# A one-core two-block kernel: gates of layer 0 in another order, and expert weights by rounded products

## The chip, the cores and the metric

The kernel runs on one core of one Trainium2 chip. The metric is the device time of one execution in microseconds (us). Five engines work beside each other: TensorE (PE, matrix products; PEld is its loading of weights), VectorE (DVE), ScalarE (ACT), GpSimd (POOL) and SyncE (SP), which issues most of the transfers. Each follows its own list of instructions, which is fixed when the program is built, and they wait for each other by semaphores.

## The reference

256 tokens of width 2048 pass a first block of two layers, then a second block. Layer 0 is attention next to a convolution, each with a gate:

```python
k, v, q, za, glu, zb = jnp.split(h @ w_in, EV_SPLITS, axis=-1)
...
attn = latent_attention(q, k, v, kc, vc)
conv = conformer_conv(glu, ev_dw_w[e], ev_dw_b[e], ev_ln_g[e], ev_ln_b[e])
mix = jnp.concatenate([attn * jax.nn.silu(za), conv * jax.nn.silu(zb)], axis=-1)
x_new = x + gate * (mix @ ev_w_out[e])
```

Layer 1 is a spatial gating unit. The second block adds a state space mixer, causal attention, and a layer of 16384 single-neuron experts, of which each token picks 8 heads x 16:

```python
q = (h @ w_q).reshape(bsz, seq, PEER_HEADS, 2, PEER_HALF_DIM)
scores = jnp.einsum('bshpd,hpnd->bshpn', q, sub_keys).astype(jnp.float32)
sv, si = lax.top_k(scores, PEER_TOPK)
...
gw = jax.nn.softmax(tv, axis=-1).astype(h.dtype)
...
a = jnp.einsum('td,ted->te', xc, expert_u[ic])
a = jax.nn.gelu(a, approximate=False) * wc
return jnp.einsum('te,ted->td', a, expert_v[ic])
```

## The kernel before

**Products.** All weights are F32 and come from DRAM in chunks of 1 MB, each half of which is 128 x 1024 numbers. ScalarE rounds a half to `whi` (fp32r, the rounded form that TensorE multiplies at full rate), VectorE makes the rest, `wlo` = raw - `whi`. The activations are split in the same way, and three rounded products make one F32 product: high by high, high by low, low by high. The text calls the products of half a chunk a half. `gemm` keeps the weights in place and streams 256 columns of tokens; `gemm_tok` keeps the tokens in place and streams 512 columns of weights; `gemm_pairs` (for `pu`, the first expert matrix) keeps the weights in place and streams high and low tokens as 512 columns for `whi`, and 256 for `wlo`.

**Order.** A planner at build time (the clock and its prices, with `SYNC`, `TICK`) calls the threads (Python generators) in turn: `add` and `post` put a thread into the plan, `fill` runs what is due after each half, `finish` runs a thread to its end there and then. A `yield "d"` hands over to VectorE's due time, `"a"` to ScalarE's, `"p1"` to TensorE's, and `"w"` waits for something else. So the order of instructions on each engine follows from prices, not from arrival at run time. The raw chunks have a ring of buffers; three `wlo` can wait unused. The long sums of the modulation vectors (`ada`) are used as filler, on TensorE (`adaps`) or on VectorE (`adaacc`).

**Layer 0.** `EV_ORDER` is the order of column groups of the first weight matrix: 1, 2, 3 are convolution input, 5 and 6 queries, 7 and 8 the gate of the convolution (`gate_b`), 9 and 10 the gate of attention (`gate_a`). A gate is computed by tokens, put through Silu by ScalarE (`szt`) and transposed by TensorE (`turn`). `attended` multiplies it into the attention result and splits that into `mixs`; `conv_ln` finishes the convolution's half. Then `evo`, the output product, runs in two passes over its inner dimension, the attention's half first. `mixed` holds the threads of the two attention groups, and `self.finish(*mixed)` stands ahead of the first evo product, `self.finish(ln)` ahead of the second pass.

**Experts.** `peer` computes the queries `pq` (four groups), scores them, and finds the 16 best of each head (`topk`, mostly VectorE). All 16384 experts are then computed densely: `pu` gives 256 x 16384 activations, which GELU and a dense matrix of weights (0 for experts not chosen) turn into `A`, and `pv` multiplies that by the second matrix. `PEER_ORDER` lists the pieces: `u` 0 to 13 first (104 halves of `pu`), then `v` 0 to 4, and so on.

The dense weights come from `expert_weights` and `weight_products`. A token's weights are a 128 x 128 matrix, the product of two one-hot matrices over its 128 choices, one of them scaled by the choice's weight. For each of 64 groups of four tokens, VectorE makes both (`oneh`, from the transposed choices `selT`: plane 1 against the numbers 0 to 127, then plane 0 with plane 2 as the weight), TensorE multiplies them into `pw`, ScalarE copies that to `wst`, and after each eight groups SP stores them to DRAM (`wd`). `weigh` loads them back by expert (`wrd`), VectorE multiplies `raw_a`, the GELU's result, by them, and ScalarE and VectorE split the product into `As`, on which `pv` waits. `RING` is how many groups of one-hot tiles may be ready. Every load `wrd` takes a slice of all eight stores, so the first one needs the last store.

In the trace every instruction stands at line 409, the helper that records it, so tiles are read by name.

## Time and profile before

| | |
|---|---|
| time, three runs | 3151.94, 3152.35, 3160.5 us; median 3152.35 |
| profiled execution | 3148.4 us, span of the core 3146.6 us |
| TensorE busy | 3080.5 us, 98% of the span |
| VectorE busy | 2263.6 us, 72% |
| ScalarE busy | 1496.6 us, 48% |
| DMA | 762.61 MB, mean 242 GB/s |
| chain that ended last | PE 90%, DVE 6%, ACT 2%, DMA 1% |

All times in what follows are of the profiled execution, counted from the start of the span. Busy time alone doesn't say what a change is worth: matrix products overlap by some hundred ns, so the distance from one start to the next is their price, not the length of one. Idle time is given with what ended it. A stretch of the chain of waits gives, in order of time, the work that nothing else could have covered.

### The profile page before, as it was taken

The numbers are of one execution on the slowest core, as the hardware profiler recorded it, in microseconds if no ns is written. First come the engines' busy times: TensorE is split into PE (matmuls) and PEld (weight loads), VectorE is DVE, ScalarE is ACT, GpSimd is POOL, SyncE is SP. The second block draws the span as 40 slices with busy tenths as digits, with TensorE's granted clock in tenths as the row PEclk, the third lists the DMA queues.
The fourth block names the chain that finished last, engine by engine and source line by source line (L and its number), as shares of the span: only waits on it lengthen the run. The fifth ranks groups of instructions, "written<-read, shape, count | busy, mean of one in ns | idle before, by whom it ended". The sixth has DMA issues, their size and how long they took to land.

```text
span 3146.6 us, 43549 instructions
## 1 busy us (share of the span) xinstructions
PE 3080.5 (98%) x17104; PEld 2562.6 (81%) x17104; DVE 2263.6 (72%) x3457; ACT 1496.6 (48%) x2044; POOL 12.7 (0%) x25
## 2 busy tenths in 40 slices
PE   6899999999999999999999999999999999999999
PEld 5666779778897777789998898888888888888887
DVE  4499879788777887868789997555566556655654
ACT  3345554445445556544445555444354444444433
POOL 0000000000000000000000000000000000000000
PEclk8999999999999999999999999999999999999999
DMA  8877786788875565777654566566566666655663
GB/s 341 331 282 256 257 308 225 280 320 316 304 291 201 221 239 185 271 276 285 243 181 174 190 239 242 208 219 207 201 242 234 228 219 250 237 207 205 232 214 134
DMA packets 140781, 762.61 MB, mean 242 GB/s; under 512 B 12624, under 2 KB 45392, under 8 KB 53920
## 3 DMA queue, kind: packets, MB, share of 16 engines
q1 hardware_dynamic: 137680, 750.83, 65.3%
q0 software_dynamic: 1744, 5.85, 0.6%
q8 instruction: 134, 2.20, 0.3%
q10 hardware_dynamic: 1152, 3.15, 0.3%
q14 instruction: 71, 0.58, 0.1%
HBM read 738.81 MB, written 20.97 MB: 241 GB/s over the span
## 4 chain that ended last, share of the span: by engine, by line
PE 90%; DVE 6%; ACT 2%; DMA 1%; issue 1%; SPq 0%; ACTq 0%; DVEq 0%
PE pv L409 25%; PE q L409 23%; PE pu L409 21%; PE ps L409 9%; PE adaps L409 3%; DVE wlo L409 2%; PE last L409 2%; PE pw L409 2%; PE S L409 1%; PE kvc L409 1%; PE kv L409 1%; DVE si L409 1%; PE po L409 1%; PE ss L409 0%; PE turn L409 0%
## 5 line engine op out<-in xcount | busy, mean ns | idle before, releaser
L409 DVE TENSOR_TENSOR wlo<-raw,whi 128x1024 fp32r<-128x1024 f32 x970 | 1177.2, 1220 | 563.4 <-PE pv L409 270.4
L409 ACT ACTIVATE whi<-raw 128x1024 fp32r<-128x1024 f32 x970 | 1022.8, 1060 | 1118.5 <-PE pv L409 396.2
L409 PE MATMUL pu<-hs,whi 128*128 128x512 f32 x2048 | 725.1, 398 | 0.0
L409 PE MATMUL q<-whi,hs 128*128 128x512 f32 x1984 | 643.6, 397 | 3.9 <-DVE ypad L409 3.9
L409 PE MATMUL pv<-whi,As 128*128 128x512 f32 x2048 | 633.6, 390 | 0.8 <-DVE y L409 0.8
L409 PE MATMUL pu<-hs,wlo 128*128 128x256 f32 x2048 | 574.7, 281 | 1.2 <-DVE wlo L409 1.2
L409 PEld LDWEIGHTS q<-whi,hs 128*128 128x128 f32 x1984 | 373.5, 188 | 120.6 <-issue 34.1
L409 PEld LDWEIGHTS pu<-hs,whi 128*128 128x128 f32 x2048 | 384.6, 188 | 91.0
L409 PEld LDWEIGHTS pv<-whi,As 128*128 128x128 f32 x2048 | 384.5, 188 | 81.6 <-DVE y L409 1.2
L409 PE MATMUL pv<-wlo,As 128*128 128x512 f32 x1024 | 398.4, 389 | 0.0
L409 PE MATMUL q<-wlo,hs 128*128 128x512 f32 x992 | 388.5, 392 | 0.9 <-DVE wlo L409 0.9
L409 PEld LDWEIGHTS pu<-hs,wlo 128*128 128x128 f32 x2048 | 386.8, 189 | 2.8 <-DVE wlo L409 2.6
L409 DVE SCALAR_TENSOR_TENSOR adaacc<-raw,silc,adaacc 128x1024 f32<-128x1024 f32 x176 | 221.2, 1280 | 101.8 <-DMA raw<-in_ada_dram 101.7
L409 PEld LDWEIGHTS pv<-wlo,As 128*128 128x128 f32 x1024 | 192.3, 188 | 40.9 <-issue 1.0
L409 PEld LDWEIGHTS q<-wlo,hs 128*128 128x128 f32 x992 | 187.1, 189 | 39.7 <-DVE wlo L409 3.3
L409 PE MATMUL ps<-hs,whi 128*128 128x256 f32 x768 | 152.3, 298 | 21.8 <-ACT hs L409 17.0
L409 PE MATMUL ps<-mixs,whi 128*128 128x256 f32 x832 | 154.7, 288 | 0.0
L409 PEld LDWEIGHTS ps<-hs,whi 128*128 128x128 f32 x768 | 126.8, 202 | 29.3 <-ACT hs L409 21.1
L409 PEld LDWEIGHTS ps<-mixs,whi 128*128 128x128 f32 x832 | 132.5, 196 | 3.5 <-issue 3.4
L409 PE MATMUL ps<-mixs,wlo 128*128 128x256 f32 x416 | 119.1, 286 | 0.0
L409 PE MATMUL ps<-hs,wlo 128*128 128x256 f32 x384 | 113.0, 294 | 1.2 <-DVE wlo L409 1.2
L409 DVE SCALAR_TENSOR_TENSOR cacc<-ypad,pk,cacc 128x256 f32<-128x256 f32 x240 | 99.3, 477 | 0.0
(382 smaller groups left out, 3045.6 us busy)
## 6 DMA issues: line engine op xcount, KB each, us to landing
raw<-in_ada_dram SPq DMA_DIRECT2D x160, 1024.0 KB, 5.2
raw<-in_pu_dram SPq DMA_DIRECT2D x128, 1024.0 KB, 4.9
raw<-in_pv_dram SPq DMA_DIRECT2D x128, 1024.0 KB, 4.8
raw<-in_w_dram SPq DMA_DIRECT2D x60, 1024.0 KB, 4.8
raw<-in_od_dram SPq DMA_DIRECT2D x48, 1024.0 KB, 6.8
raw<-in_ev_dram SPq DMA_DIRECT2D x44, 1024.0 KB, 5.4
raw<-in_ada0s_dram SPq DMA_DIRECT2D x32, 1024.0 KB, 7.9
raw<-in_evo_dram SPq DMA_DIRECT2D x16, 1024.0 KB, 5.2
```

The source lines that it names most:

```text
L409: r = f(*args, **kw)
```

## The change

Four edits. (1) In layer 0 the attention gates (9, 10) are computed ahead of the convolution's gates (7, 8), and the mixture is a `LazySplit`: each part is finished when the first product that reads it is written down, not ahead of all. (2) In `gemm_pairs` each half does its eight products with `whi`, then its eight with `wlo`, instead of alternating. (3) `pq` is computed by tokens (`gemm_tok`, 384 products of 512 columns instead of 768 of 256), copied out by ScalarE, transposed by TensorE (32 transposes) and copied again. (4) The one-hot tiles are rounded numbers now: 0 and 1 are exact, and the weight is split into a rounded part (plane 3) and the rest (plane 2). VectorE makes four tiles of 128 x 512 for four tokens: `oneh`, the unscaled `onew`, and its products with the two weight planes, both of which read the unscaled tile, the second in place. TensorE does two rounded products of 128 columns for each token instead of one F32 product. `RING` falls from 4 to 2.

```diff
@@ -173,10 +173,10 @@
 PEER_ORDER = (("u", 0, 13), ("v", 0, 4), ("v", 4, 8), ("v", 8, 12), ("u", 13, 20), ("v", 12, 18), ("u", 20, 26), ("v", 18, 24),
               ("u", 26, 32), ("v", 24, 32))
 SPARE = 2
-RING = 4
+RING = 2
 LAG = 2
 GATE_AT = 120
-EV_ORDER = (1, 2, 5, 6, 3, 7, 8, 9, 10)
+EV_ORDER = (1, 2, 5, 6, 3, 9, 10, 7, 8)
 
 
 def make_plan():
@@ -691,12 +691,11 @@
         for kc in range(n_kc):
             for j in range(2):
                 hi, lo = (t.rearrange("p a (b n) -> p (a b) n", n=256) for t in self.take(name, g, kc, j))
-                for a in range(4):
-                    kt = 8 * kc + 4 * j + a
-                    for n in range(2):
-                        s = slice(n * 128, n * 128 + 128)
-                        self.mm(ps[:, n], hi[:, a, s], act.hl(kt), start=(kt == 0), stop=False, skip_group_check=True)
-                        self.mm(ps[:, n, 1, :], lo[:, a, s], act.h(kt), start=False, stop=(kt == 8 * n_kc - 1), skip_group_check=True)
+                part = [(a, n, 8 * kc + 4 * j + a, slice(n * 128, n * 128 + 128)) for a in range(4) for n in range(2)]
+                for a, n, kt, s in part:
+                    self.mm(ps[:, n], hi[:, a, s], act.hl(kt), start=(kt == 0), stop=False, skip_group_check=True)
+                for a, n, kt, s in part:
+                    self.mm(ps[:, n, 1, :], lo[:, a, s], act.h(kt), start=False, stop=(kt == 8 * n_kc - 1), skip_group_check=True)
                 self.fill()
         return ps
 
@@ -1235,7 +1234,7 @@
                 heads.append(self.add(self.attn0(4 * g + j, qT[g][:, j, :], kT, V, at[g][:, j, :], [t] + tk, st), 2))
 
         szb = [None] * 2
-        mix = Split()
+        mix = LazySplit(self)
 
         def silu(t, ps):
 
@@ -1260,7 +1259,7 @@
 
         def gate_a(g):
             p = gates(9 + g)
-            mixed.append(self.post(p, attended(g, p)))
+            mix.th[g] = [self.post(p, attended(g, p))]
 
         def attended(g, p):
             sza = self.ar("sza")
@@ -1270,7 +1269,6 @@
             yield "a"
             yield from self.split(mix, g, at[g], "mix")
 
-        mixed = []
         for e in EV_ORDER:
             if e < 4:
                 glu(e)
@@ -1282,13 +1280,12 @@
                 gate_a(e - 9)
             if len(conv) == 4 and ln is None:
                 ln = self.add(self.conv_ln(conv, cacc, szb, mix), 1)
+                mix.th[2] = mix.th[3] = [ln]
         self.params = self.add(self.ssm_params(), 8)
         self.wait_plan((0, 2, 0))
-        self.finish(*mixed)
         for g in range(4):
             ps = self.gemm("evo", g, EVO_PASSES[0], mix)
             self.post(ps, self.gated(g, ps, self.mods[0, 2, 0]), eng="d")
-        self.finish(ln)
         self.out_proj("evo", mix, self.mods[0, 2, 0], EVO_PASSES[1])
         self.dump_x("x1")
 
@@ -1978,13 +1975,20 @@
         tk = []
 
         def evict(q, ps):
-            nc.scalar.activation(q, ps, AF.Copy)
+            s = self.ar("pqs", F32, (128, 2, 512))
+            nc.scalar.activation(s, ps, AF.Copy)
+            for j in range(2):
+                yield "p1"
+                pt = self.turn_in(s[:, :, 256 * j:256 * j + 256])
+                yield "a"
+                nc.scalar.activation(q[:, 2 * j:2 * j + 2, :], pt, AF.Copy)
             yield "p"
 
         for g in range(4):
-            ps = self.gemm("pq", g, range(4), h)
+            p = self.acc("q", (128, 2, 512))
+            self.gemm_tok("pq", g, range(4), [h], [[p[:, 0, :], p[:, 1, :]]])
             q = self.ar("pqT")
-            t = self.post(ps, evict(q, ps))
+            t = self.post(p, evict(q, p))
             tk.append(self.add(self.topk(g, q, t, sk[g // 2], sel, tk[-1:]), 5))
         wt = self.add(self.expert_weights(tk, sel), 5)
         A = LazySplit(self)
@@ -2178,7 +2182,7 @@
 
         nc = self.nc
         yield from self.after(tk)
-        cols = self.ar("selT", F32, (128, 3, 256))
+        cols = self.ar("selT", F32, (128, 4, 256))
         for w in range(3):
             yield "p1"
             pt = self.ms("selp", (128, 256))
@@ -2189,19 +2193,22 @@
         yield "d"
         io = self.cst("iota")
 
-        ring = [self.ar("oneh", F32, (128, 2, 4, 128)) for _ in range(RING)]
+        nc.scalar.activation(cols[:, 3, :].bitcast(F32R), cols[:, 2, :], AF.Copy)
+        nc.vector.tensor_sub(cols[:, 2, :], cols[:, 2, :], cols[:, 3, :])
+        ring = [(self.ar("oneh", F32R, (128, 4, 128)), self.ar("onew", F32R, (128, 2, 4, 128))) for _ in range(RING)]
         made, used = [], []
         out = self.add(self.weight_products(ring, made, used), 4)
         for i in range(64):
             while i - len(used) >= RING:
                 yield "w"
             yield "d", 0.0
-            o, t = ring[i % RING], 4 * i
-            nc.vector.tensor_tensor(o[:, 0], io[:, None, :].to_broadcast([128, 4, 128]), cols[:, 1, t:t + 4, None].to_broadcast([128, 4, 128]),
-                                    op=ALU.is_equal)
-            for j in range(4):
-                nc.vector.tensor_scalar(o[:, 1, j, :], io, cols[:, 0, t + j:t + j + 1], cols[:, 2, t + j:t + j + 1],
-                                        op0=ALU.is_equal, op1=ALU.mult)
+            (o, ow), t = ring[i % RING], 4 * i
+            wide = lambda w: cols[:, w, t:t + 4, None].to_broadcast([128, 4, 128])
+            every = io[:, None, :].to_broadcast([128, 4, 128])
+            nc.vector.tensor_tensor(o, every, wide(1), op=ALU.is_equal)
+            nc.vector.tensor_tensor(ow[:, 0], every, wide(0), op=ALU.is_equal)
+            nc.vector.tensor_tensor(ow[:, 1], ow[:, 0].bitcast(F32), wide(2), op=ALU.mult)
+            nc.vector.tensor_tensor(ow[:, 0], ow[:, 0].bitcast(F32), wide(3), op=ALU.mult)
             made.append(self.clock.t["dve"])
         yield from self.after([out])
 
@@ -2213,10 +2220,11 @@
             while len(made) <= i:
                 yield "w"
             yield "p1", made[i]
-            o = ring[i % RING]
+            o, ow = ring[i % RING]
             pw = self.ms("pw", (128, 4, 128))
             for j in range(4):
-                self.mm(pw[:, j, :], o[:, 0, j, :], o[:, 1, j, :], start=(j == 0), stop=True, skip_group_check=True)
+                for z in range(2):
+                    self.mm(pw[:, j, :], o[:, j, :], ow[:, z, j, :], start=(j == 0 and z == 0), stop=z == 1, skip_group_check=True)
             used.append(i)
             yield "a"
             for q in range(4):
```

Three places in the order of instructions. First TensorE at the end of layer 0, where the last gate's products `q` end and `evo` (`ps<-mixs`) begins; before:

```order
L409 MATMUL q<-wlo,hs 128x512
L409 MATMUL q<-whi,hs 128x512
L409 MATMUL turn<-sc,szt 128x128 x8
L409 MATMUL ps<-mixs,whi 128x256 x2
L409 MATMUL ps<-mixs,wlo 128x256
```

and after, at the same place and then four halves further on:

```order
L409 MATMUL q<-wlo,hs 128x512
L409 MATMUL q<-whi,hs 128x512
L409 MATMUL ps<-mixs,whi 128x256 x2
L409 MATMUL ps<-mixs,wlo 128x256
...
L409 MATMUL adaps<-raw,silc_105 32x512 x4
L409 MATMUL turn<-sc,szt 128x128 x8
L409 MATMUL ps<-mixs,whi 128x256 x2
```

The eight transposes have moved behind the first four halves of evo; over the layer `adaps` has 152 products instead of 160, and VectorE four more additions `adaacc`.

Second, VectorE while the one-hot tiles are made, two groups before:

```order
L409 TENSOR_TENSOR oneh<-sc,selT 128x512
L409 TENSOR_SCALAR oneh<-sc,selT 128x128 x4
L409 TENSOR_TENSOR oneh<-sc,selT 128x512
L409 TENSOR_SCALAR oneh<-sc,selT 128x128 x4
L409 TENSOR_TENSOR wlo<-raw,whi 128x1024
```

and two groups after:

```order
L409 TENSOR_TENSOR oneh<-sc,selT 128x512
L409 TENSOR_TENSOR onew<-sc,selT 128x512
L409 TENSOR_TENSOR onew<-onew,selT 128x512 x2
L409 TENSOR_TENSOR wlo<-raw,whi 128x1024
L409 TENSOR_TENSOR oneh<-sc,selT 128x512
L409 TENSOR_TENSOR onew<-sc,selT 128x512
L409 TENSOR_TENSOR onew<-onew,selT 128x512 x2
L409 TENSOR_TENSOR wlo<-raw,whi 128x1024
```

A `wlo`, one for each half of `pu`, now stands behind each group instead of each second one; from the first one-hot tile to the last there are 66 `wlo` and 17 `raw_a<-pu,pul` of 128x512, before 32 and 8.

Third, TensorE at the end of the weights: before, the last product `pw` and what follows,

```order
L409 MATMUL pw<-oneh 128x128 x8
L409 MATMUL pu<-hs,whi 128x512
L409 MATMUL pu<-hs,wlo 128x256
L409 MATMUL pu<-hs,whi 128x512
L409 MATMUL pu<-hs,wlo 128x256
```

with 36 halves of `pu` up to the first `pv<-whi,As`; and after:

```order
L409 MATMUL pw<-onew,oneh 128x128 x8
L409 MATMUL pu<-hs,whi 128x512 x8
L409 MATMUL pu<-hs,wlo 128x256 x8
L409 MATMUL pw<-onew,oneh 128x128 x8
L409 MATMUL pu<-hs,whi 128x512 x8
L409 MATMUL pu<-hs,wlo 128x256 x8
L409 MATMUL pv<-whi,As 128x512
L409 MATMUL pv<-wlo,As 128x512
```

The first `pw` stands behind 37 halves of `pu` now (36 before), the last ahead of half 104 (ahead of half 69 before), so that one half is left in front of `pv`.

## Rows read from the trace of the kernel before

**Rows 1.** Table of stretches, us: busy time (instructions) by engine, granted clock, DMA share, GB/s.
```profile
core 0: us, PE busy (x) PEld busy (x) DVE busy (x) ACT busy (x) POOL busy (x), PEclk, DMA share, GB/s
440.00:460.00 20.00, 13.91 (x67) 11.29 (x60) 13.21 (x12) 7.74 (x9) 0.00 (x0) 0.88 0.97 382
1764.00:1911.00 147.00, 147.00 (x1029) 135.77 (x1028) 145.91 (x357) 87.91 (x300) 0.00 (x0) 1.00 0.60 216
```

**Rows 2.** Timeline of TensorE around 451 to 459: start, us, instructions [idle before <-releaser].
```profile
451.17 0.39 PE L409 MATMUL q<-whi,hs 128*128 128x512 f32 x1
457.65 1.97 PE L409 MATMUL turn<-sc,szt 128*128 128x128 f32 x8 [6.09 <-ACT szt L409]
```

**Rows 3.** Chain of waits at the end of layer 0: start, us, what.
```profile
447.29 7.29 DMA raw<-in_evo_dram
...
455.64 1.04 ACT whi L409
456.68 0.92 ACT szt L409
...
459.62 4.00 PE ps L409 x24
463.61 0.99 PE adaps L409 x8
```

**Rows 4.** Chain of waits in the retrieval stage, at its first halves and transposes.
```profile
1552.33 5.68 PE ps L409 x24
...
1577.87 0.44 PE xtp L409 x4
1578.30 2.88 PE ps L409 x24
```

**Rows 5.** Chain of waits while the expert weights are made, and at the first long pv.
```profile
1770.12 2.78 PE pu L409 x16
1772.89 1.78 PE pw L409 x16
...
2010.97 261.16 PE pv L409 x1152
```

**Rows 6.** Costliest groups: line, operation xcount | busy, mean ns | idle before, releaser.
```profile
L409 PE MATMUL pu<-hs,wlo 128*128 128x256 f32 x2048 | 574.7, 281 | 1.2 <-DVE wlo L409 1.2
```

**Rows 7.** Timeline of VectorE while one-hot tiles are made.
```profile
1807.43 1.21 DVE L409 TENSOR_TENSOR wlo<-raw,whi 128x1024 fp32r<-128x1024 f32 x1
1808.57 0.67 DVE L409 TENSOR_TENSOR oneh<-sc,selT 128x512 f32<-128x512 f32 x1
1809.17 1.10 DVE L409 TENSOR_SCALAR oneh<-sc,selT 128x128 f32<-128x128 f32 x4
1810.20 0.67 DVE L409 TENSOR_TENSOR oneh<-sc,selT 128x512 f32<-128x512 f32 x1
```

**Rows 8.** Timeline of VectorE in the top-k stretch; the second eq reads the first.
```profile
1696.54 1.22 DVE L409 TENSOR_TENSOR eq<-abf,sc 128x1024 f32<-128x1024 f32 x1
1697.79 1.22 DVE L409 TENSOR_TENSOR eq<-eq,sif 128x1024 f32<-128x1024 f32 x1
1698.93 1.22 DVE L409 TENSOR_TENSOR wlo<-raw,whi 128x1024 fp32r<-128x1024 f32 x1
```

**Rows 9.** End of the weights: chain of waits, then timelines of ScalarE, SP and VectorE.
```profile
1909.33 1.78 PE pw L409 x16
...
1910.26 1.68 ACT L409 ACTIVATE wst<-pw 128x128 f32<-128x128 f32 x8 [1.94 <-PE pw L409]
...
1911.46 3.54 SPq L409 DMA_DIRECT2D wd<-wst  x4
...
1916.65 7.52 SPq L409 DMA_DIRECT2D wrd<-wd  x4
...
1924.37 1.22 DVE L409 TENSOR_TENSOR raw_a<-raw_a,wrd 128x1024 f32<-128x1024 f32 x1
...
1926.64 1.29 DVE L409 TENSOR_TENSOR As<-raw_a,As 128x512 fp32r<-128x512 f32 x2
```

**Rows 10.** From issue to landing of the tiles wrd, then wd, last line of each tile's view.
```profile
DMA to landing us min/median/max: 5.9/7.2/9.6
DMA to landing us min/median/max: 3.7/6.8/10.1
```

## The prediction

> **What bounds the kernel now.** I read the table of stretches first: columns of busy time by engine, then the granted clock and the DMA share. From 1764 to 1911, the stretch in which the expert weights are made, TensorE is busy 147.00 of 147.00 us and VectorE 145.91: two engines with no slack between them [rows 1]. At the end of layer 0 (440 to 460) TensorE is busy only 13.91 of 20 us, and the DMA share is 0.97 [rows 1]. The chain of waits and the timeline say what stood there: the last `q` product starts at 451.17 and the next instruction of TensorE, the transposes `turn<-sc,szt`, at 457.65, 6.09 us idle until ScalarE's `szt` [rows 2]; `szt` itself stood behind the split of an evo chunk that landed only 7.29 us after it was asked for [rows 3]. Everywhere else that the diff touches, TensorE is the chain. So a product saved counts in full where TensorE leads; in the weights' stretch it counts only if VectorE gets shorter too.
>
> **Layer 0: gates in another order, mixture finished on demand.** Before, all of the mixture had to be ready ahead of evo's first product, and the eight last transposes stood in between. After, TensorE goes from the last `q` straight into `ps<-mixs`; the transposes come four halves later, behind work that covers ScalarE. A half is one half of a 1 MB weight chunk, 24 products here. What can go: the idle 6.25 us (0.39 us product to 457.65, less its regular 0.23), of which I leave 0.7 for the first pair of groups becoming ready; the first half ran 4.00 us, where a later one takes 2.88 [rows 3, 4], so 1.1 for the lower of the clock's two levels, 1.2 GHz, after the idle time (the granted clock is 0.88 of 2.4 GHz on the mean of that stretch and 1.00 where TensorE never pauses [rows 1]); the transposes 1.97 instead of twice 0.44 [rows 2, 4], 1.1. By the order two chunks of modulation products leave TensorE for VectorE in this layer, 0.99 each [rows 3], and VectorE has room for their four additions. Sum: −5.5 − 1.1 − 1.1 − 2.0 = **−9.7**. Bounds: −11 (nothing left of the idle time) to 0, if the transfer of the evo chunks sets the pace: the first halves need those same chunks, and with a DMA share of 0.97 they cannot come much sooner. I take the gain, since the queues have asked for the next chunks already while TensorE still works on `q`, and `szt`, not a chunk, is named as what ended the idle time [rows 2]. One more chunk of modulation leaves TensorE in a later stage: **−1.0** (0 to −1.0).
>
> **The order inside a `pu` half.** Eight 512-column products and then eight 256-column ones, instead of alternating. The count and the 2.78 us of a half [rows 5] are the same. The low parts are needed 1.8 us later, so the 1.2 us that TensorE waited for `wlo` ahead of `pu<-hs,wlo` [rows 6] goes: **−1.2** (0 to −1.2).
>
> **`pq` by tokens.** Before, 768 products of 256 columns, at 2.88/24 = 0.120 us each [rows 4] 92.2 us. After, 384 of 512 columns, at 261.16/1152 = 0.227 [rows 5] 87.2 us, and 32 transposes, at 0.44 for four [rows 4] 3.5 us, with 0.2 for the changes. **−1.3** (0 to −1.4). ScalarE gets eight more copies, beside a TensorE stretch of 90 us; they are covered, unless the last one stands ahead of the first top-k, which the transposes of one group (0.88) bound.
>
> **The expert weights on TensorE.** Each of the 64 groups of four tokens was four F32 products, which the trace shows as eight records, 16 records in 1.78 us [rows 5]; so 0.112 a record, 0.896 a group, 57.3 us in all. After, it is eight rounded products of 128 columns. The trace before has no rounded product of so few columns. Nearest rows: the record of the F32 product with the same 128 weight columns and 128 streamed columns, 0.112, below a 256-column rounded product, 0.120 [rows 4]. At 0.112 the eight cost the same 57.3: **0**. Bounds: half of 0.120 each (time by columns) gives 30.7, −26 on TensorE; 0.120 gives +4. The gain would not reach the end, for the next reason.
>
> **The expert weights on VectorE.** This term sets the sign. Before, a group took one comparison of 512 columns (0.60 from its start to the next) and four `TENSOR_SCALAR` of 128 (1.03): 1.63 us; a `wlo` takes 1.14 [rows 7]. After, it takes four operations of 512 columns, 4 × 0.602 = 2.41, and the last two are products on the tile just written; by the order each waits on the engine itself. What such a wait costs, two `eq` show: the second reads what the first wrote and starts 1.25 after it, where an operation of that size that waits for nothing follows after 1.14 [rows 7, 8]: 0.11 more. So 2.41 + 2 × 0.11 = 2.63 us a group. Between first and last weight operation VectorE now also makes 66 `wlo` (32 before) and 17 half-size additions of `raw_a`, because the planner stretches the making over 66 halves of `pu` instead of 33. That is 64 × 2.63 + 66 × 1.14 + 17 × 0.60 = **254 us** of VectorE, against 66 × 2.785 + 64 × 0.896 = **241 us** of TensorE. VectorE falls behind the plan by 13 us, of which the two weight tiles in the ring and three low-part slots absorb some 2: **+11** (8 to 14; 0 if the waits cost nothing, since 64 × 2.41 + 85 = 240). A stretch in which TensorE waits for VectorE a little in every group shows no long idle time, only many short ones.
>
> The Trainium skill, page "VectorE: DVE Perf Modes", section "Rules for kernel authors", says to minimise the count of chained operations and not the semaphores between them; by it the waits would be free and the term 0. The trace disagrees here: 1.25 against 1.14.
>
> **The end of the making.** Before, 36 halves of `pu` (100 us) lay between the last `pw` and the first `pv` that needs the weights; by the order only one half (2.78) is left. The weights' way there: the last `pw` ends at 1911.12, ScalarE copies out, SP stores `wd`, then loads `wrd` (issued at 1916.65), VectorE multiplies `raw_a` by it at 1924.37 at the latest, and the pair `As` follows, with its first low tile ready at about 1927.3 [rows 9]: 16.2 us. VectorE was busy with another `raw_a` until 1924.4, so the transfer may have landed up to 2 us before; 14.3 is what I take. Minus 2.8 covered: **+11.5**. Bounds: +10 with the shortest landings, +17 with the longest of `wd` and `wrd` [rows 10]. By the order SP has one `pv` chunk between the store and the load; it waits for the split of an earlier chunk, which needs no weights. TensorE has nothing else in its order to fill that time. After it, the lower clock level again: the first half after a wait in the retrieval stage took 5.68 against 2.88, the one in layer 0 4.00 [rows 3, 4]: **+2.5** (1.1 to 2.8), nearer the long one, since this pause is the longest.
>
> **Sum.** −9.7 − 1.0 − 1.2 − 1.3 + 0 + 11 + 11.5 + 2.5 = +11.8. The profiled execution took 3148.4, the median of the runs 3152.35, 3.95 above it. So 3160.2 on its own basis and **3164** on that of the median.
>
> **The rivals.**
> Rival 1, not slower: VectorE keeps pace, because the waits on its own results cost nothing with these shapes. It decides at 2.43 us a group: below that, VectorE's sum is under TensorE's 241. For it: 2.41 is just under; the ring lets each engine run ahead. Against it: the `eq` pair. The +11 goes and the end of the making stays: −13.2 + 14.0 = +0.8, **3153**.
> Rival 2: a rounded product of 128 columns costs as much as a wide one, 0.227 [rows 5], since nothing of this form was in the trace. Then 512 × 0.227 = 116 instead of 57, TensorE's sum is 300 and VectorE's no longer counts: +59 in place of +11, **3212**. Against it: the price follows the columns from 512 to 256.
> Rival 3, the change doesn't do what it says: the gain of layer 0 stays out, because evo's chunks arrive at the rate of a DMA share of 0.97 [rows 1] whatever TensorE does first. The time is then +21.5, **3174**.
>
> **How the numbers follow.** Forecast 0.48, rival 1 0.22, rival 3 0.13, rival 2 0.12, and 0.05 for something faster than these (an end of the making that VectorE's pace hides in part, with layer 0 gaining all of its 11). A difference under 0.3% (9.4 us) is about what a measurement of this kernel can't tell from no change, so the borders are 3143 and 3162. The forecast lies just above the upper one; a third of it falls below. Same: 0.14 of the forecast and the 0.22 of rival 1, 0.36. Faster: 0.07. Slower: 0.57. The range leaves out rival 2 and the farthest faster cases: below, rival 1 with VectorE's ring absorbing a little, 3148; above, rival 3 with the upper bounds of the end, 3183.
>
> **What would show each step.** In layer 0: no idle time of 6 us between the last `q` and the first `ps`. In the weights' stretch: VectorE busy without a gap for about 254 us, TensorE with short waits of 10 to 13 us in sum, named for `onew` or `wlo`; a `pw` group of eight in 0.9 us. At its end: one idle time of about 11 us on TensorE before `pv<-whi,As`, ended by `As`, then a half at the lower clock. Wrong would be: `pw` groups of over 1 us or under 0.6; multiplications of `onew` that start 0.60 after what they read; a first `pv` that starts without a pause, which would mean that the exchange through DRAM is off the path.

## The result and the profile after

The changed kernel takes 3184.42 us, median of 5 runs (3181.46 to 3185.79), the kernel before on the same chip 3159.03 (5 runs, 3151.94 to 3165.43): ratio 1.0082, interval 1.007 to 1.0095, so 22 to 30 us slower. The forecast was 3164 on 3152, 12 us slower; the direction held, the size is doubled, and 3184 lies above the range. The kernel before itself was 6.7 us slower here than in the three runs of the forecast; counted from 3152, 25.4 more is 3178. So leaving the range is in part that shift; that the difference is twice the forecast is not.

The profiled executions differ by more, 3185.79 to 3148.4. That of before is among the fastest of its kernel: its first `q` product starts at 165.7 us, in all 13 other traces of this case between 169.0 and 173.7, though nothing ahead of it differs in what is computed. I therefore compare stages, not ends. The starts of the first products of a stage, read from the traces (us; "weights alone" and "first edit alone" are experiments below, and the former has layers 0 and 1 of the kernel before):

| first ... | before | weights alone | first edit alone | after |
|---|---|---|---|---|
| `q` (layer 0) | 165.7 | 170.3 | 170.3 | 171.7 |
| `ps<-mixs` (evo) | 459.3 | 463.8 | 453.4 | 453.9 |
| `pv<-whi,hs` (layer 1) | 571.6 | 576.2 | 576.8 | 578.6 |
| `pu` | 1656.9 | 1661.2 | 1665.7 | 1671.1 |
| `pv<-whi,As` | 2010.8 | 2040.1 | 2019.6 | 2050.8 |
| last `pv` | 3141.3 | 3172.4 | 3148.7 | 3178.6 |

Two readings. From the first `pu` to the first `pv` that needs the weights it is 353.9 us before and 379.7 after, 25.8 more: this is where the loss is made. And evo starts 10 us earlier with the edit, yet layer 1 starts later: what layer 0 gains is given back within 120 us. Counted from the first `q`, layer 1 starts after 405.8 us before, 406.5 with the first edit alone and 406.9 after.

First the weights. The timeline of VectorE in the changed kernel (start, us, instructions), the counterpart of [rows 7]:

```profile
1898.69 1.22 DVE L409 TENSOR_TENSOR wlo<-raw,whi 128x1024 fp32r<-128x1024 f32 x1
1899.82 0.68 DVE L409 TENSOR_TENSOR oneh<-sc,selT 128x512 fp32r<-128x512 f32 x1
1900.43 0.68 DVE L409 TENSOR_TENSOR onew<-sc,selT 128x512 fp32r<-128x512 f32 x1
1901.15 1.42 DVE L409 TENSOR_TENSOR onew<-onew,selT 128x512 fp32r<-128x512 f32 x2
1902.48 0.69 DVE L409 TENSOR_TENSOR oneh<-sc,selT 128x512 fp32r<-128x512 f32 x1
```

A group takes 1902.48 - 1899.82 = 2.66 us: 0.60, then 0.72 up to the first product, which reads the tile just written, and 1.33 for the two products. From its first one-hot tile to its last VectorE takes 254.5 us, where the forecast had 254. TensorE goes from the first `pw` to the last in 253.1 us, with 66 halves at 2.793 and 57.3 of `pw` in it, 241.6: it waits 11.4. Part of that the view of costliest groups shows on the `pw` products themselves (count | busy, mean ns | idle before):

```profile
L409 PE MATMUL pw<-onew,oneh 128*128 128x128 f32 x512 | 67.4, 274 | 6.0 <-DVE onew L409 6.0
L409 PE MATMUL pv<-whi,As 128*128 128x512 f32 x2048 | 635.9, 391 | 13.3 <-ACT As L409 12.5
```

The second of these rows is the end of the making. The timelines of TensorE, SP, VectorE and ScalarE there, the counterpart of [rows 9], and in a second block the first half of `pv` in the chain of waits:

```profile
2034.33 1.08 PE L409 MATMUL pw<-onew,oneh 128*128 128x128 f32 x8
...
2035.75 2.75 SPq L409 DMA_DIRECT2D wd<-wst  x4
2039.82 9.05 SPq L409 DMA_DIRECT2D wrd<-wd  x4
...
2048.83 1.23 DVE L409 TENSOR_TENSOR raw_a<-raw_a,wrd 128x1024 f32<-128x1024 f32 x1 [8.67 <-DMA wrd<-wd]
...
2050.09 1.15 ACT L409 ACTIVATE As<-raw_a 128x512 fp32r<-128x512 f32 x2 [9.27 <-DVE raw_a L409]
...
2050.77 0.80 PE L409 MATMUL pv<-whi,As 128*128 128x512 f32 x1 [12.53 <-ACT As L409]
```

```profile
2050.77 5.29 PE pv L409 x12
```

One half of `pu` covers the beginning, and then TensorE stands for 12.5 us while the last weights go through DRAM. The half after it takes 5.29 us instead of 12 x 0.227 = 2.72, with a granted clock of 0.53 from 2050.8 to 2056.0: the 1.2 GHz level again.

Now layer 0. The table of stretches (busy time by engine, granted clock, DMA share, GB/s), and in a second block TensorE's timeline and ScalarE's, the counterparts of [rows 1 to 3]:

```profile
460.00:470.00 10.00, 6.93 (x58) 5.89 (x56) 7.26 (x21) 2.13 (x3) 4.38 (x6) 1.00 1.02 285
470.00:480.00 10.00, 7.16 (x40) 6.69 (x44) 8.32 (x32) 5.13 (x7) 0.00 (x0) 0.66 0.78 296
```

```profile
465.87 1.06 PE L409 MATMUL adaps<-raw,silc 128*32 128x512 f32 x8
472.84 1.97 PE L409 MATMUL turn<-sc,szt 128*128 128x128 f32 x8 [5.91 <-ACT szt L409]
...
462.41 2.01 ACT L409 ACTIVATE whi<-raw 128x1024 fp32r<-128x1024 f32 x2 [2.90 <-DMA raw<-in_evo_dram]
469.87 2.00 ACT L409 ACTIVATE whi<-raw 128x1024 fp32r<-128x1024 f32 x2 [5.45 <-DMA raw<-in_evo_dram]
471.78 1.00 ACT L409 ACTIVATE szt<-q 128x1024 f32<-128x1024 f32 x1
```

The pause has not gone, it has moved 15 us on: the transposes of the last gate, which is now the convolution's, wait 5.91 us for their `szt`. Its input was complete at 454, when the last `q` ended, but on ScalarE it stands behind four evo chunks, of which the fourth landed at 469.9. Before, it stood behind two, and started at 456.59 (ScalarE's timeline before):

```profile
447.91 2.01 ACT L409 ACTIVATE whi<-raw 128x1024 fp32r<-128x1024 f32 x2 [6.04 <-DMA raw<-in_evo_dram]
454.68 2.00 ACT L409 ACTIVATE whi<-raw 128x1024 fp32r<-128x1024 f32 x2 [4.76 <-DMA raw<-in_evo_dram]
```

A second pause, 2.2 us before, is 6.3 us now, at the border of the two layers, by the same pattern (timelines of ScalarE and TensorE):

```profile
567.79 1.06 ACT L409 ACTIVATE whi<-raw 128x1024 fp32r<-128x1024 f32 x1 [10.02 <-DMA raw<-in_od_dram]
568.76 1.32 ACT L409 ACTIVATE sq<-x 128x256 f32<-128x256 f32 x4
...
569.21 3.57 PE L409 MATMUL ss<-onefg,sq 128*128 128x1 f32 x16 [6.29 <-ACT sq L409]
```

ScalarE waits 10 us for the second chunk of layer 1, which SP requested at 560.97, and the squares for the norm, whose input was ready at 563.8, stand behind it. Before, they stood ahead of it (ScalarE's timeline and TensorE's before):

```profile
559.45 0.81 ACT L409 ACTIVATE sq<-x 128x256 f32<-128x256 f32 x2 [0.62 <-DVE x L409]
...
571.90 1.99 ACT L409 ACTIVATE whi<-raw 128x1024 fp32r<-128x1024 f32 x2
...
560.92 0.92 PE L409 MATMUL ss<-ones,sqr 128*128 128x1 f32 x4 [2.03 <-DVE sqr L409]
```

### The profile page after: what moved, and what is told of

Its sections match the earlier page's. It is cut to its first block, busy times and chain, and to the rows that moved or that the text cites. A ratio compares the mean times of both kernels' runs of the same rounds, so it can differ in the third digit from the quotient of the medians.

```text
span 3184.0 us, 42723 instructions
## 1 busy us (share of the span) xinstructions
PE 3086.3 (97%) x16728; PEld 2555.7 (80%) x16728; DVE 2324.8 (73%) x3400; ACT 1495.0 (47%) x2053; POOL 12.7 (0%) x25
## 4 chain that ended last, share of the span: by engine, by line
PE 59%; DVE 11%; issue 2%; ACT 1%; DMA 0%; DVEq 0%; SPq 0%; ACTq 0%
PE pv L409 22%; PE pu L409 16%; PE q L409 12%; DVE wlo L409 4%; PE ps L409 4%; DVE onew L409 3%; PE last L409 1%; DVE oneh L409 1%; PE adaps L409 1%; PE S L409 0%; DVE raw_a L409 0%; DMA wrd<-wd 0%; PE bu L409 0%; DVE x L409 0%; DVE si L409 0%
## 5 line engine op out<-in xcount | busy, mean ns | idle before, releaser
L409 PE MATMUL q<-whi,hs 128*128 128x512 f32 x2240 | 725.6, 397 | 6.3 <-DVE ypad L409 3.9
L409 PE MATMUL pv<-whi,As 128*128 128x512 f32 x2048 | 635.9, 391 | 13.3 <-ACT As L409 12.5
L409 PEld LDWEIGHTS q<-whi,hs 128*128 128x128 f32 x2240 | 421.9, 188 | 133.2 <-issue 31.1
L409 PE MATMUL pu<-hs,whi 128*128 128x512 f32 x2048 | 516.7, 394 | 0.0
L409 PE MATMUL q<-wlo,hs 128*128 128x512 f32 x1120 | 439.2, 392 | 2.9 <-DVE wlo L409 2.7
L409 PEld LDWEIGHTS pu<-hs,wlo 128*128 128x128 f32 x2048 | 279.0, 190 | 21.1 <-DVE wlo L409 0.9
L409 PE MATMUL pu<-hs,wlo 128*128 128x256 f32 x2048 | 285.4, 282 | 0.1
L409 PEld LDWEIGHTS q<-wlo,hs 128*128 128x128 f32 x1120 | 211.4, 189 | 47.8 <-DVE wlo L409 6.9
L409 ACT ACTIVATE wst<-pw 128x128 f32<-128x128 f32 x256 | 50.0, 282 | 109.6 <-PE pw L409 109.6
L409 DVE TENSOR_TENSOR onew<-onew,selT 128x512 fp32r<-128x512 f32 x128 | 88.6, 692 | 4.4
L409 ACT ACTIVATE raw_a<-raw_a 128x512 f32<-128x512 f32 x64 | 40.6, 635 | 104.6 <-DVE raw_a L409 104.6
```

What stands on the lines that cost most here:

```text
L409: r = f(*args, **kw)
```

## The experiments

Each was timed against the kernel before on the same chip; the times are medians in us.

| label: kernel | this | before | ratio | interval |
|---|---|---|---|---|
| e1_ev: first edit alone | 3160.77 | 3154.99 | 1.0017 | 1.0003 to 1.0031 |
| e2_pairs: second alone | 3148.34 | 3154.99 | 0.9977 | 0.9964 to 0.999 |
| e3_pq: third alone | 3156.85 | 3154.99 | 1.0003 | 0.999 to 1.0016 |
| e4_weights: fourth alone | 3180.95 | 3154.99 | 1.0082 | 1.0062 to 1.0102 |
| e7_evo: first, evo chunks rounded late | 3151.08 | 3154.2 | 0.9987 | 0.9975 to 0.9999 |
| e8_evo_od: and layer 1's | 3155.84 | 3154.2 | 1.0003 | 0.9992 to 1.0013 |
| e9_best: and the second edit | 3146.98 | 3154.2 | 0.9973 | 0.9964 to 0.9983 |
| e10_u14: changed, 14 groups of `pu` first | 3168.64 | 3154.2 | 1.0044 | 1.0027 to 1.0061 |
| e11_evo_pairs: evo chunks late, second edit | 3141.53 | 3156.58 | 0.9961 | 0.9947 to 0.9975 |
| e12_between: 14 groups, comparison between | 3169.07 | 3156.58 | 1.0041 | 1.0027 to 1.0055 |
| e13_apart: and tiles apart | 3162.75 | 3155.06 | 1.002 | 1.001 to 1.0031 |
| e14_priced: 15 groups, wait priced | 3163.44 | 3155.06 | 1.0025 | 1.0013 to 1.0038 |

### The four edits, one at a time

First edit:

```diff
-EV_ORDER = (1, 2, 5, 6, 3, 7, 8, 9, 10)
+EV_ORDER = (1, 2, 5, 6, 3, 9, 10, 7, 8)
...
-        mix = Split()
+        mix = LazySplit(self)
```

> The kernel before with the first edit alone: attention gates ahead of the convolution's gates, mixture finished on demand. My forecast's step (the pause of 6.25 us goes, transposes are covered, two modulation chunks leave TensorE): 10 to 11 us faster than before. The rival (the pause only moves behind the first halves of evo, because the transposes' input stands on ScalarE behind a chunk that the full DMA queues deliver late; two such pauses are in the trace of the changed kernel, 6.5 us at 466 and 6.5 us at 563): no gain, 0 to 10 us slower than before.

Measured: 1 to 10 us slower, the ratio's middle 5.4. The rival, not my step. In its trace TensorE waits 5.15 us for `szt`, until 471.7, and 5.68 us for `sq`, until 567.5, as in the changed kernel. Up to the first product of layer 1 the trace shows only 0.7 us of the loss. The rest lies further on, and no trace tells it from noise: from there to the last product of block 2's output it is 978.6 us, before 975.0, but e2_pairs, e3_pq and e4_weights, whose TensorE lists there are those of before, take 975.6, 981.7 and 974.4.

Second edit:

```diff
-                for a in range(4):
...
+                for a, n, kt, s in part:
+                    self.mm(ps[:, n], hi[:, a, s], act.hl(kt), start=(kt == 0), stop=False, skip_group_check=True)
+                for a, n, kt, s in part:
+                    self.mm(ps[:, n, 1, :], lo[:, a, s], act.h(kt), start=False, stop=(kt == 8 * n_kc - 1), skip_group_check=True)
```

> The kernel before with the second edit alone: in each half of pu all products with the high weights first, then all with the low. My forecast's step: 1.2 us faster (one wait for wlo goes, the price of a half stays 2.78). The rival (products of one width in a row are cheaper than alternating ones: a half takes 2.793 in the trace of the changed kernel where it took 2.826 before): 256 halves by 0.033, with the 1.2 some 9 to 10 us faster.

Measured: 3 to 11 us faster, middle 7.3. The chains of waits over the same 56 halves, of before and of this kernel:

```profile
2272.13 158.28 PE pu L409 x896
```

```profile
2274.96 156.40 PE pu L409 x896
```

A half takes 158.28/56 = 2.826 us alternating and 156.40/56 = 2.793 in rows of one width. From start to start, a 512-column product and a 256-column one behind it take 0.237 + 0.117 us when they alternate; 0.2305 and 0.119 when they stand among their own kind. But alternation doesn't have that price everywhere. The 36 halves between the last `pw` and the first `pv`, in the chains of before, e7_evo and e2_pairs:

```profile
1911.12 99.85 PE pu L409 x576
```

```profile
1914.90 101.76 PE pu L410 x576
```

```profile
1913.25 100.57 PE pu L409 x576
```

Alternating takes 2.774 a half in the first (0.230 + 0.117) and 2.827 in the second, in the same order; grouped it is 2.794, between the two. What decides which of its two prices alternation takes is not shown. So 0.033 holds for the 152 later halves, 5.0 us, and not for all 256; from the first `pu` to the last `pv` it is 1478.0 us here, and 1483.0 to 1486.3 in before, e1_ev, e7_evo and e8_evo_od, which alternate.

Third edit:

```diff
...
-            ps = self.gemm("pq", g, range(4), h)
+            p = self.acc("q", (128, 2, 512))
+            self.gemm_tok("pq", g, range(4), [h], [[p[:, 0, :], p[:, 1, :]]])
```

> The kernel before with the third edit alone: pq by tokens with transposes. My forecast: 1.3 us faster (0 to 1.4). By the traces of both kernels from the end of the last product of block 2's output to the first pu: 0.3 us faster. Rival: the copies and transposes delay the top-k and with it the weights, 2 us slower or more.

Measured: between 3 us faster and 5 slower; neither my 1.3 nor zero can be told from it. The traces say more. From the last product of block 2's output to the first `pw` it is 220.2 us, in before 217.9 and in e1_ev, whose TensorE list there is that of before, also 217.9: some 2.3 slower. TensorE waits 1.64 us for a `wlo` in the third group, and then for the last transposed queries (timelines of ScalarE and TensorE):

```profile
1676.38 0.26 ACT L409 ACTIVATE tv<-tv 128x64 f32<-128x64 f32 x1 [3.49 <-DVE tv L409]
1676.54 0.58 ACT L409 ACTIVATE pqT<-turn 128x512 f32<-128x512 f32 x1
...
1677.17 2.50 PE L409 MATMUL sco<-sk,pqT 128*128 128x128 f32 x20 [1.27 <-ACT pqT L409]
```

The copy `pqT` stands on ScalarE behind `tv`, a step of the top-k that waits for VectorE: the pattern of layer 0 again.

Fourth edit:

```diff
-RING = 4
+RING = 2
...
-            for j in range(4):
-                nc.vector.tensor_scalar(o[:, 1, j, :], io, cols[:, 0, t + j:t + j + 1], cols[:, 2, t + j:t + j + 1],
-                                        op0=ALU.is_equal, op1=ALU.mult)
...
+            nc.vector.tensor_tensor(ow[:, 0], every, wide(0), op=ALU.is_equal)
+            nc.vector.tensor_tensor(ow[:, 1], ow[:, 0].bitcast(F32), wide(2), op=ALU.mult)
+            nc.vector.tensor_tensor(ow[:, 0], ow[:, 0].bitcast(F32), wide(3), op=ALU.mult)
```

> The kernel before with the fourth edit alone: the expert weights from rounded one-hot tiles, four VectorE operations of 512 columns a group, eight products of 128 columns. My forecast's terms: 11 for VectorE's pace, 11.5 for the end of the making and 2.5 for the clock after it, 25 us slower than before. Rival, that the rounded products or the ring of 2 cost more by themselves: over 30. If the order of the pu products matters to it (alternating here), 1 to 3 us more or less.

Measured: 20 to 32 us slower, middle 25.9, where the forecast's terms say 25. The four middles add up to 5.4 - 7.3 + 0.9 + 25.9 = 25, the whole of the change, as far as intervals of 4 to 6 us to either side can say.

### What holds the layer 0 gain back

The planner may put the rounding of a chunk into ScalarE's list up to 6 us (`ARRIVE`) before it counts on the chunk. The first edit with that margin taken away for evo, in the first 600 us:

```diff
+SOON = {'evo': 0.0}
...
-        if not force and self.clock.used(raw.tensor.name) > self.clock.t["pe"] + ARRIVE:
+        if not force and self.clock.used(raw.tensor.name) > self.clock.t["pe"] + SOON.get(it[1], ARRIVE) * (self.clock.t["pe"] < 600) + ARRIVE * (self.clock.t["pe"] >= 600):
```

> The first edit alone (as in e1_ev), and up to 600 us of planned time the planner puts the rounding of an evo chunk into ScalarE's order only when it counts the chunk as landed, not up to 6 us earlier. So the last gate's szt stands behind one evo chunk instead of four. Theory that the order of ScalarE's queue makes the pause: the 5.7 us ahead of the transposes and the low clock behind it go, 5 to 9 us faster than e1_ev, which was 5.4 slower than before. Rival, that the transfer of the evo chunks sets the pace (DMA share 0.96 to 1.01 there): the pause shows up at a later product that waits for wlo of evo, within 2 us of e1_ev.

Measured: 0 to 8 us faster than before, middle 4.1, so by the middles 9.5 better than the edit as it was. ScalarE's timeline and TensorE's, and in a second block the table of stretches:

```profile
452.88 2.01 ACT L410 ACTIVATE whi<-raw 128x1024 fp32r<-128x1024 f32 x2 [7.29 <-DVE adaacc L410]
454.79 1.00 ACT L410 ACTIVATE szt<-q 128x1024 f32<-128x1024 f32 x1
...
457.99 0.60 PE L410 MATMUL turn<-sc,szt 128*128 128x128 f32 x4
```

```profile
460.00:470.00 10.00, 9.49 (x77) 8.31 (x76) 9.48 (x24) 4.33 (x7) 4.38 (x6) 1.00 1.01 305
470.00:480.00 10.00, 8.77 (x67) 7.19 (x66) 7.83 (x23) 3.60 (x5) 0.00 (x0) 1.00 0.99 389
```

`szt` stands behind one evo chunk, the transposes wait for nothing, and the granted clock stays at 1.00, though the DMA share is as high as before. So it was mainly the order of ScalarE's list, not the rate of the transfers. A remnant of the rival is there: TensorE waits for `wlo` nine times between 455 and 554, 5.8 us in all and none over 1.03, where e1_ev waits 11.3 from evo to layer 1. And the edit moves more than `szt`: the transposes now come in two fours, after one and after two halves of evo. The later pause went as well: the shifted order leaves only chunks ahead of the squares that were requested by 539.8, and the second chunk of layer 1, requested at 562.0, is rounded at 571.1, behind them.

The same for layer 1's chunks, with 2 us more: they are put in only 2 us after the planner counts them as landed.

```diff
-SOON = {'evo': 0.0}
+SOON = {'evo': 0.0, 'od': -2.0}
```

> As e7_evo, and the same for the chunks of layer 1's first weights, so that ScalarE squares the last part of x at the end of layer 0 ahead of the rounding of the first of these chunks, as in the kernel before. Theory: the 5.8 us pause at 562 of e1_ev becomes the 2.2 us of the kernel before, some 3 to 4 us faster than e7_evo. Rival: the chunk is needed right after and sets the start of layer 1 anyway, 0 to 1 us.

Measured: between 3 us faster than before and 4 slower. Not better than without it; the medians are 4.8 apart the other way. The timeline of TensorE shows where the chunk is missed now:

```profile
571.54 0.50 PE L410 MATMUL pv<-wlo,hs 128*128 128x512 f32 x1 [0.76 <-DVE wlo L410]
575.68 0.51 PE L410 MATMUL pv<-whi,hs 128*128 128x512 f32 x1 [1.35 <-ACT whi L410]
576.94 0.79 PE L410 MATMUL pv<-wlo,hs 128*128 128x512 f32 x1 [0.76 <-DVE wlo L410]
600.48 0.80 PE L410 MATMUL pv<-wlo,hs 128*128 128x512 f32 x1 [2.70 <-DVE wlo L410]
```

Layer 1 starts 2.5 us ahead of e7_evo's and is 5.4 behind it 30 us later. The first three waits, 2.9 us, are the chunk: its rounding now stands behind the new activations `hs`. The fourth is the same pattern on VectorE, where `wlo` stands behind a filler that waits for its transfer:

```profile
596.81 2.48 DVE L410 SCALAR_TENSOR_TENSOR adaacc<-raw,silc,adaacc 128x1024 f32<-128x1024 f32 x2 [3.69 <-DMA raw<-in_ada_dram]
599.21 3.49 DVE L410 TENSOR_TENSOR wlo<-raw,whi 128x1024 fp32r<-128x1024 f32 x3
```

Rounding too late costs time as well as rounding too early.

That kernel with the second edit:

> e8_evo_od with the second edit (grouped pu products), the weights and pq of the kernel before. If the theories of e7_evo and e8_evo_od hold, the gain of e2_pairs (7 us) adds to theirs: 10 to 17 us faster than before. If the rivals hold, layer 0 stays a loss of 5 and the sum is 0 to 4 us faster.

Measured: 5 to 11 us faster than before, middle 8.5, at the lower end of what I expected; its trace has the same four waits, 5.6 us. Without the part for layer 1:

> e7_evo with the second edit (grouped pu products): the two gains found so far, 4 us of e7_evo and 7 us of e2_pairs. If they add, 11 us faster than before (7 to 16), and a little ahead of e9_best; if the pauses of layer 0 only move on, 7 us.

Measured: 8 to 17 us faster than before, middle 12.3. The two gains add, and this is faster than both kernels of the case: 3141.53 us.

### What the weights cost

More cover at the end:

```diff
-PEER_ORDER = (("u", 0, 13), ("v", 0, 4), ("v", 4, 8), ("v", 8, 12), ("u", 13, 20), ("v", 12, 18), ("u", 20, 26), ("v", 18, 24),
+PEER_ORDER = (("u", 0, 14), ("v", 0, 4), ("v", 4, 8), ("v", 8, 12), ("u", 14, 20), ("v", 12, 18), ("u", 20, 26), ("v", 18, 24),
```

> The changed kernel with 14 instead of 13 groups of pu ahead of the first pv, so that nine halves instead of one lie between the last pw and the first pv that needs the weights, all else of the making alike. My forecast's terms for the end: 11.5 of pause and 2.5 of clock go, 14 us faster than the changed kernel, so about 11 slower than before. Rival, that the pause is a transfer that the pu products don't cover or that the later pv lose it again: under 5 us faster than the changed kernel.

Measured: 9 to 19 us slower than before, middle 13.9, where the changed kernel is 25.9 slower by the same ratio: 12 us better. The row of the costliest groups that showed 13.3 us ahead of `pv<-whi,As` now has 0.8:

```profile
L409 PE MATMUL pv<-whi,As 128*128 128x512 f32 x2048 | 634.0, 390 | 0.8 <-DVE y L409 0.8
L409 PE MATMUL pw<-onew,oneh 128*128 128x128 f32 x512 | 67.5, 275 | 6.9 <-DVE onew L409 6.9
```

What is left is 14; by the table below 12.6 of it is TensorE waiting at VectorE's pace. The wait for the operation just before, taken out by putting the other comparison between:

```diff
-            nc.vector.tensor_tensor(o, every, wide(1), op=ALU.is_equal)
             nc.vector.tensor_tensor(ow[:, 0], every, wide(0), op=ALU.is_equal)
+            nc.vector.tensor_tensor(o, every, wide(1), op=ALU.is_equal)
```

> e10_u14 with the two comparisons of a group in the other order, so that the comparison of oneh stands between the unscaled onew and the products that read it; same four operations. Theory, that a wait for the operation just before costs 0.12 us each time and VectorE sets the pace of the making: a group takes 2.54 instead of 2.66 us, 64 of them 7 to 8 us, so about 6 us slower than before where e10_u14 is 14 slower. Rival, that the wait costs nothing or that something else sets the pace: within 2 us of e10_u14.

Measured: 13 us slower than before, as its parent. The expectation failed in the time, not in the operation; VectorE's timeline:

```profile
1851.37 0.69 DVE L409 TENSOR_TENSOR onew<-sc,selT 128x512 fp32r<-128x512 f32 x1
1851.97 0.69 DVE L409 TENSOR_TENSOR oneh<-sc,selT 128x512 fp32r<-128x512 f32 x1
1852.57 1.42 DVE L409 TENSOR_TENSOR onew<-onew,selT 128x512 fp32r<-128x512 f32 x2
1853.90 0.69 DVE L409 TENSOR_TENSOR onew<-sc,selT 128x512 fp32r<-128x512 f32 x1
```

A group takes 2.53 instead of 2.66 us, and the making is 15 us shorter. But the planner, which prices the operations, has put the groups closer together too: 61 halves of `pu` beside them instead of 66. From starts of products and of one-hot tiles (us; the products' own time is halves x 2.793 + 57.3):

| kernel | first `pw` to last | halves | products' own time | TensorE waits | VectorE, first tile to last |
|---|---|---|---|---|---|
| changed | 253.1 | 66 | 241.6 | 11.4 | 254.5 |
| 14 groups first | 254.2 | 66 | 241.6 | 12.6 | 255.6 |
| comparison between | 239.3 | 61 | 227.7 | 11.7 | 240.7 |
| tiles apart | 231.0 | 61 | 227.7 | 3.3 | 232.4 |
| wait priced | 260.6 | 71 | 255.6 | 5.0 | 264.8 |

The wait is the same 12: VectorE's part got 15 us shorter, and with five halves fewer the products beside it 14. New theory: TensorE's list is written for the durations that the planner has, and what VectorE takes longer than that is waited for, group by group. The planner counts the wait of a read after a write (0.13), but none for the product in place, which overwrites what the one before it has just read, and that too starts 0.72 after it. 64 x 0.12 = 7.7 us in both kernels. Two tests of it, one that takes the operation's wait away, and one that leaves the operation and tells the planner.

```diff
...
-            nc.vector.tensor_tensor(ow[:, 1], ow[:, 0].bitcast(F32), wide(2), op=ALU.mult)
-            nc.vector.tensor_tensor(ow[:, 0], ow[:, 0].bitcast(F32), wide(3), op=ALU.mult)
+            nc.vector.tensor_tensor(ow[:, 1], o[:, 1].bitcast(F32), wide(2), op=ALU.mult)
+            nc.vector.tensor_tensor(ow[:, 0], o[:, 1].bitcast(F32), wide(3), op=ALU.mult)
```

> As e12_between, and the unscaled one-hot tile stands in a place of its own, so that neither product overwrites what the other has just read: no operation of a group waits for the one just before it. In e12_between VectorE's making got 15 us shorter and the time did not move; TensorE waited as long as in e10_u14. Theory: TensorE's waits are what VectorE takes longer than the planner has priced, 0.13 us a group in both (the wait of the product in place, 0.12, is not in its prices), 64 groups 8 to 9 us; with that wait gone too the lag is gone, 7 to 9 us faster than e12_between, 4 to 6 slower than before. Rival, that the waits of TensorE come from elsewhere (the ring of 2, the products by themselves): within 2 us of e12_between.

Measured: 3 to 10 us slower than before, middle 6.3, by the ratios 6.6 better than its parent; TensorE's waits fall from 11.7 to 3.3. VectorE's timeline:

```profile
1855.90 1.29 DVE L409 TENSOR_TENSOR oneh<-sc,selT 128x512 fp32r<-128x512 f32 x2
1857.10 1.29 DVE L409 TENSOR_TENSOR onew<-oneh,selT 128x512 fp32r<-128x512 f32 x2
1858.31 1.22 DVE L409 TENSOR_TENSOR wlo<-raw,whi 128x1024 fp32r<-128x1024 f32 x1
```

A group takes 2.41, and no operation waits. The other test:

```diff
             nc.vector.tensor_tensor(ow[:, 0], ow[:, 0].bitcast(F32), wide(3), op=ALU.mult)
+            self.clock.t["dve"] += 0.14
```

with 15 groups of `pu` first, so that the end stays covered.

> e10_u14 with the instructions of a group unchanged, but the planner's clock of VectorE set 0.14 us further after each group, so that it spreads the groups as VectorE will really deliver them (71 halves of pu beside them instead of 66), and 15 groups of pu ahead of the first pv, to keep the end covered. Theory as for e13_apart: the operations are as long as in e10_u14, but TensorE no longer waits for them: 6 to 9 us faster than e10_u14, 5 to 8 slower than before. Rival, that the price of the operations themselves is what costs: within 2 us of e10_u14.

Measured: 4 to 12 us slower than before, middle 7.9, some 6 better than with 14 groups alone, within what the two intervals leave open; the waits fall from 12.6 to 5.0 with the same instructions. The theory holds in both: in the last one the operations are as long as ever, and most of TensorE's waits are gone. What the two still lose to the kernel before, 6 to 8 us, I did not take apart; 3 to 5 of it are the waits that are left, and the first three edits, which both contain, come to -1 by their middles. Some of the waits left may be TensorE's own price: by the planner's formula a `pw` product costs as much as one of 256 columns, 0.120, where it takes 0.112, and 512 x 0.008 are 4 us. No run tests that.

## Why the prediction was wrong in its size

**Layer 0, -9.7 and -1.0: measured +5.4 (first edit alone).** This step failed. I put the transposes "behind work that covers ScalarE" and took the place on TensorE from the order, but did not look at where their input stands on ScalarE: behind four chunks of evo, where before there were two. Evo's start did come 10 us earlier, as worked out, and then the pause came back, because `szt` now stands behind the last of these four, which landed at 469.9. The sentence that it was `szt`, not a chunk, that ended the idle time was a misreading of [rows 2]: the chain in [rows 3] already showed the chunk ahead of `szt`, and the prediction's first paragraph says so. My third rival ("the gain stays out") had the right result and the wrong cause, the DMA share: with the share as high and the order put right, 4 of the 10 us are there (0 to 8). On top of it came a loss that I had not looked for, 4 us at the border of the layers. The traces bear out that the gain stays out (0.7 us slower up to layer 1); that it is a loss of 5 only the times say, with 1 to 10.

**`pu` halves, -1.2: measured -7.3 (-11 to -3).** The step "the count and the 2.78 us of a half are the same" failed. [rows 5] show one half of 2.78, and in that trace the 36 halves behind the making go at that price too; but the 152 later ones take 2.826, and grouping makes all of them 2.793. The saving hung on a difference of 1%, in 152 halves, which one half read from one place could not show.

**`pq`, -1.3.** The times don't decide it: +1, interval -3 to +5. By the traces, one of each kernel, it is +2.3, and the step "they are covered" failed: two waits, 1.64 and 1.27 us, outweigh what the wider products save. The bound of 0.88 had the transposes in it, but not where their copy stands on ScalarE.

**The weights, 0 + 11 + 11.5 + 2.5 = 25: measured 25.9 (20 to 32).** Each part has its row. On TensorE the product of 128 columns takes 0.112 us from start to start (median in the changed kernel's trace), as assumed, so the second rival (0.227) is out. VectorE's group was 2.63 and took 2.66; the predicted wait of 10 to 13 us is 11.4. The pause was 11.5 and is 12.5, the half after it costs 2.6 more, 2.5 predicted; with the pause covered 12 came back, of 14. The reason given for the 2.5, that the longest pause brings the longest time at the lower clock, does not follow from the rows: the half of 5.68 came behind waits of 1.20 and 1.53 us, the one of 4.00 behind 6.09. There the size was right by luck. The mechanism, VectorE's time less the products' beside it, holds in all five kernels of the table: VectorE is the longer one each time, and TensorE waits for the difference less 1 to 4 us; with the tiles apart VectorE is 8.3 shorter beside the same 61 halves, and the wait 8.4. The ring of 2 was not varied by itself; the kernel with the tiles apart has it too and waits only 3.3. What I had not seen is that the planner chooses how many halves stand beside, by its own prices. So a faster operation that it also prices as faster gains nothing (comparison between), and what it has not priced is what TensorE waits for. The first rival, that the waits cost nothing, is out. The Trainium skill, page "VectorE: DVE Perf Modes", section "Rules for kernel authors", advises to minimise the count of chained operations, not the semaphores; by that the group with the comparison between would be as long as its parent's. The trace disagrees, 2.53 against 2.66 us.

**Sum.** Forecast +11.8, measured +25.4. By the middles of the single edits, each with 4 to 6 us to either side, 13.1 of the difference of 13.6 are layer 0 (+16.1), `pu` (-6.1), `pq` (+2.2) and the weights (+0.9). The upper end of the range had rival 3's layer 0 at zero; it did not allow for layer 0 as a loss.

## What to carry to other kernels

When an instruction is moved on one engine, follow its inputs on the engines that make them: in a list that is fixed in advance, work that is ready stands behind work that waits for a transfer, and the pause moves with it. If a planner writes the lists, a wait that it does not price is paid by the engine that is planned to need the result, and a faster operation helps TensorE only as far as its price does not fall with it. Before the last result of a long making is needed, leave its whole way (here 15 us through DRAM) covered by other work.

## What the runs showed that I had not expected

- A 512-column and a 256-column product in alternation have two prices for the pair, 0.347 and 0.354 us (2.774 and 2.826 for 16), each kept over many halves, and the same stretch of the list has either in the traces of two kernels; among their own kind they take 0.3495 (2.793). What decides between the two is open.
- An operation of VectorE that overwrites what the one before it has just read starts 0.72 us after it, like one that reads what the other has just written. With another operation between the writing and the reading, or with the places of the products apart, each starts 0.60 after the one before it.
- Executions of the same first stage differ by several us: the first `q` starts at 165.7 in one trace and up to 173.7 in others, so that two profiled executions should be compared stage by stage.
